# A trunk of two decoder layers on one core: the order of copies, low parts and differences in the last round of the down projection

## The chip, the cores and the metric

The kernel runs on one core of a Trainium2 chip. The core's engines work side by side, each through its own list of instructions in a fixed order: TensorE (PE in the profile) multiplies matrices, VectorE (DVE), ScalarE (ACT) and GpSimd (POOL) do elementwise work, and SyncE (SP) issues the transfers. An engine that waits at the head of its list holds up everything behind it. The metric is the time of one execution in device microseconds, as the median of several runs.

## The reference

The model has a Mamba-2 layer and a layer of stick-breaking attention. Each is followed by a gated feed-forward block (FFN). Only the end of that block, its down projection, is touched here. It takes 2816 features of about 1040 tokens to 1024 features, once in each layer.

```python
D_MODEL = 1024
SEQ = 1024
D_FF = 256 * ((8 * D_MODEL // 3 + 255) // 256)   # 2816

def _conv_ffn(u, w_up, conv_w, conv_b, w_down):
    h = _causal_dwconv(u @ w_up, conv_w, conv_b)
    g, val = jnp.split(h, 2, axis=-1)
    return (jax.nn.silu(g) * val) @ w_down

def reference(x, ...):
    ...
        h = h + _conv_ffn(_rmsnorm(h, ffn_norm[layer]), ffn_w_up[layer], ffn_conv_w[layer],
                          ffn_conv_b[layer], ffn_w_down[layer])
    return _rmsnorm(h, final_norm)[:, N_META:]
```

## The kernel before

**Three products for one.** Every operand in float32 is kept as a high part, which is a rounded copy made on ACT, and a low part, which is the operand less the high part. `mm3` (lines 194 to 200) multiplies high by high (L198), high by low (L199) and low by high (L200) into one bank of PSUM. The low part of a weight is made on POOL by `pieces` in four instructions of 256 columns (all on L99); the low part of the tokens' operand is made on DVE.

**The down projection.** The 22 blocks of 128 features are treated in two ways. Sixteen blocks go through a scheme that makes a two by two block product out of seven smaller ones, after sums and differences of the operands (products 1, 2, 7, 6, 5, 3, 4 in this order). There are two rounds, and a round has two sets (`Set`) of two feature blocks in each half. A product is multiplied for the first set and then for the second into the same banks, and after the second set DVE adds each bank to its running sum in `add` (L1383; in the first round ACT copies some of them). Layer 0 has 1040 tokens: a product there has eight tiles of 260 columns, which take all eight banks. Layer 1 has 1024 tokens (the meta tokens are gone): four tiles of 512 columns, so that two products fit in the banks. The other six blocks, the "plain rows" (`rows`), are multiplied in the usual way behind the last product: for the first quarter of the tokens (`j == 0`) all six rows go into the eight banks at once (`wide_first`), and then DVE adds them to the stream on L1467.

**The operands.** `operands(i)` makes what a product needs of one set. DVE forms a sum or difference of weights or of tokens (L1320, output `w` or `b`). ACT copies the weights' high part (`wh`, L1327) and the tokens' high part (`gh`, L1329). POOL makes `wl`; DVE makes `gl` (L1330). Product 4 has one difference, of tokens (b21 less b11). `make` calls this one set ahead of the multiplication in the program's text. The tiles `wh` and `wl` have three buffers each, so the last product's operands can be copied only when TensorE has left a product in front.

**The plain rows' operands.** `weights(b, hi, lo)` loads a row's weights into a `w32` tile (L1390), copies the high part on ACT (L1391), and makes the low part on POOL. Row 0 and row 1 take the buffers `fh` and `fl`, in which the second set's raw weights lie, row 2 an `x32` tile, row 3 two large tiles, and rows 4 and 5 `wh` and `wl`. `w32` has three buffers. Row 0 is called at product 3, the others at product 4. `tokens(0)` loads the six rows' tokens of the first half (L1401), copies their high part on ACT (L1402, output `g`), and makes the low part on DVE (L1403). `tokens(1)` does it for the second half behind the first quarter.

**The sums.** When all seven products are there, `sums` puts them together into the result in 28 additions on DVE (L1349), each asked for by `next(work)`: two behind each of the six plain rows of the first quarter, then one behind each of the eight feature tiles of the second and third quarters. In layer 0 POOL also scales and splits the first weights of the attention (`first_key`, `load_w`, lines 176 to 185) while this goes on.

**What sets the order.** Outside the attention a planner orders the instructions of each engine, and the queue of transfers too. It goes by the place of an instruction in the program's text and by times that it models, and it hands out a tile's buffers as they come free in these modelled times. `behind(a, b, reason)` ties `a` behind `b` in that order. A tie between instructions of one engine adds no wait of its own to the program; it fixes which comes first.

Of the kernel before, what the change touches and what calls it, by code (L numbers as in the profile page):

```python
# [13 lines left out]
P = 128  # L14
# [75 lines left out]
def pieces(eng, out, x, y, op):  # L90

    n = out.shape[1]
    size = 1
    for d in out.shape[2:]:
        size *= d
    step = max(1, PIECE // size)
    for a in range(0, n, step):
        c = slice(a, min(a + step, n))
        eng.tensor_tensor(out[:, c], x[:, c], y[:, c], op=op)  # L99


class Trunk:
# [1168 lines left out]
    def down(self, layer, gd, hd, pool, after, each=None):  # L1271
# [9 lines left out]
        half = lambda j: slice(S - S * j, 2 * S - S * j)  # L1281

        behind = self.behind
        lows = []

        def behind_low(ins, n):

            if len(lows) >= n:
                behind(ins, lows[-n], "behind the low part in front")
# [4 lines left out]
        class Set:  # L1294
# [16 lines left out]
            def operands(me, i):  # L1311

                b, w = me.b, me.w
                b11, b12, b21, b22 = b[0, 0], b[0, 1], b[1, 0], b[1, 1]
                a11, a12, a21, a22 = w[0, 0], w[0, 1], w[1, 0], w[1, 1]
                a = {7: (a21, a11, a21, SUB), 6: (a21, a22, a21, SUB), 5: (a11, a11, a21, ADD), 3: (a21, a12, a21, SUB)}.get(i)
                b = {7: (b12, b22, b12, SUB), 6: (b11, b11, b12, ADD), 5: (b12, b22, b11, SUB), 4: (b11, b21, b11, SUB)}.get(i)
                for x, n in ((a, 2), (b, 1)):
                    if x:
                        d = tt(*x[:3], op=x[3])  # L1320
# [6 lines left out]
                nc.scalar.activation(wh, y, AF.Copy)  # L1327
                pt(wl, y, wh.bitcast(F32), op=SUB)
                nc.scalar.activation(gh, x, AF.Copy)  # L1329
                lows.append(tt(gl, x, gh.bitcast(F32), op=SUB))  # L1330
                return gh, gl, wh, wl

# [44 lines left out]
        def add(i, f, t, ps, first):  # L1377
            s0, n = wide[t]
            x = acc[i, f][:, s0 : s0 + n]
            if first and i in (1, 5, 6, 7):  # L1380
                nc.scalar.activation(x, ps[:, :n], AF.Copy)
            else:
                self.last_add = tt(x, x, ps[:, :n], op=ADD)  # L1383

        rows = range(2 * NW, KF)
        ws, us = [], {}

        def weights(b, hi, lo):
            w32 = self.wp.tile([P, 1024], F32, tag="w32", name=self.nm("w32"))
            nc.sync.dma_start(w32, a["w_down"][layer, b])  # L1390
            nc.scalar.activation(hi, w32, AF.Copy)  # L1391
            pt(lo, w32, hi.bitcast(F32), op=SUB)
            ws.append((hi, lo))

        def tokens(x):

            us[x] = []
            for b in rows:
                t = self.Q("g", F32R)
                hi, lo = t[:, :S], t[:, QW // 2 : QW // 2 + S]  # L1400
                nc.sync.dma_start(lo.bitcast(F32), gd[b, :, S * x : S * x + S])  # L1401
                nc.scalar.activation(hi, lo.bitcast(F32), AF.Copy)  # L1402
                low = tt(lo, lo.bitcast(F32), hi.bitcast(F32), op=SUB)  # L1403
# [18 lines left out]
        for m in range(0, len(plan), 2):  # L1422
            r, i, _ = plan[m]
            last = r + 1 == len(rounds)
            ps = {}
            if r == 0 and i == 2:
                for f in range(KD):
                    nc.sync.dma_start(h[f][:, : 2 * S] if f < 4 else h[f][:, half(0)], hd[f] if f < 4 else hd[f, :, half(0)])
            if last and i == 4:
                h22 = [self.Q("h22") for _ in range(2)]  # L1430
                h22 = [h22[f // 2][:, f % 2 * S : f % 2 * S + S] for f in range(4)]
                for f in range(4):
                    nc.sync.dma_start(h22[f], hd[4 + f, :, half(1)])
            for x in range(2):
                make(m + x + 1)
                if last and i == 3 and x:
                    weights(rows[0], *own())
                if last and i == 4 and not x:
                    tokens(0)
                    weights(rows[1], *own())  # L1440
                    weights(rows[2], *(pool.tile([P, QW], F32R, tag="x32", name=self.nm(z))[:, :D] for z in ("wh", "wl")))
                    weights(rows[3], *(self.Q(z, F32R)[:, :D] for z in ("wh", "wl")))
                    for b in rows[4:]:
                        weights(b, *common())
                for n, (t, f) in enumerate((t, f) for t in range(len(wide)) for f in range(4)):
                    if x == 0:
                        ps[t, f] = kinds[(m // 2 * 4 * len(wide) + n) % 8]("acc")
                    part(ps[t, f], made[m + x], f, t, x == 0)
                    if x == 1:
                        add(i, f, t, ps.pop((t, f)), r == 0)  # L1450
                del made[m + x]
        banks = cycle((self.mm, self.mm, self.ex, self.lg, self.lg))
        res, work = None, sums()
        for j in range(4):
            out = h if j > 1 else h[:4] + h22
            wide_first = [bank("acc") for bank in kinds] if j == 0 else []
            for i, (hi, lo) in enumerate(us[0] if j == 0 else ()):
                for f, ps in enumerate(wide_first):
                    wh, wl = (w[:, f * P : f * P + P] for w in ws[i])
                    self.mm3(ps[:, :FN], wh, wl, hi[:, :FN], lo[:, :FN], i == 0, i == len(ws) - 1)  # L1460
                ahead = token_lows[min(i + 2, len(ws) - 1)]
                for _ in range(2):
                    next(work, None)
                ahead = None
            for f in range(KD):
                if j == 0:
                    self.last_add = tt(out[f][:, :FN], out[f][:, :FN], wide_first[f][:, :FN], op=ADD)  # L1467
# [467 lines left out]
```

## Time and profile before

| what | before |
|---|---|
| median of 3 runs | 2886.41 us (2883.43 to 2888.3) |
| the profiled execution's own time | 2883.7 us |
| its span, first to last instruction | 2882.0 us |
| PE busy | 2828.9 us, 98% of the span |
| DVE busy | 2093.5 us, 73% |
| ACT, POOL busy | 1629.0 us, 57%; 1622.6 us, 56% |
| mean granted TensorE clock | 0.997 |

The profile was taken in one execution of its own. Rows of the timeline give the start from the beginning of the span in us, the duration in us, the engine, the line of the program, the operation, the output and inputs by their names with shapes, and the count where like neighbours are merged; in square brackets stands how long the engine was idle ahead of the row, and what ended that. TensorE's matmuls overlap in the record: one of 260 columns is shown with 0.28 us, but the next starts 0.12 us after it, so the time of a stretch is read from starts. A few per cent of the matmul records can be missing.

### The profile page before, as it was taken

What the parts mean: (1) busy time and instruction counts of PE and PEld (TensorE: products, weight loads), DVE (VectorE), ACT (ScalarE), POOL (GpSimd) and SP (SyncE); (2) the same over time, 40 slices, a digit from 0 to 9 for tenths busy, and PEclk for the clock granted to TensorE, in tenths of its full rate; (3) what the DMA queues carried; (4) which work ended last, traced back from release to release, by engine and by line L of the source; (5) the groups of instructions that cost most, each with busy time, mean ns of one, the idle gap of its engine ahead of it and who ended that gap; (6) DMA issues with size and microseconds to landing.
All of it is one profiled execution on the core that took longest, in us unless ns stands there. A gap on an engine that the chain in (4) does not pass through costs nothing. (4 is left out here: it accounts for less than half of the span.)

```text
span 2882.0 us, 58690 instructions
## 1 busy us (share of the span) xinstructions
PE 2828.9 (98%) x21859; PEld 2712.8 (94%) x21859; DVE 2093.5 (73%) x4068; ACT 1629.0 (57%) x3393; POOL 1622.6 (56%) x2440
## 2 busy tenths in 40 slices
PE   8999999999999999999999999999999999999998
PEld 7989999999999999999999999999798999999888
DVE  5676666668596767676886888888759676667776
ACT  5555454543265655555335888887736555565433
POOL 2366455643529888868843222222363888886872
PEclk9999999999999999999999999999999999999999
DMA  4233334333412222244132222221332222225331
GB/s 118 85 112 99 112 87 134 104 131 104 131 55 97 76 80 80 78 169 156 53 121 72 65 62 69 62 59 53 135 117 76 80 82 81 75 81 183 110 103 67
DMA packets 135674, 274.51 MB, mean 95 GB/s; under 512 B 15859, under 2 KB 68220, under 8 KB 135388
## 3 DMA queue, kind: packets, MB, share of 16 engines
q1 hardware_dynamic: 129764, 259.60, 28.7%
q0 software_dynamic: 2048, 6.49, 0.6%
q10 hardware_dynamic: 3576, 4.67, 0.5%
q8 instruction: 172, 2.82, 0.4%
q14 instruction: 114, 0.93, 0.1%
HBM read 204.63 MB, written 51.16 MB: 89 GB/s over the span
## 5 line engine op out<-in xcount | busy, mean ns | idle before, releaser
L99 POOL TENSOR_TENSOR wl<-w,wh 128x256 fp32r<-128x256 f32 x768 | 685.0, 922 | 366.5 <-ACT wh L185 268.0
L198 PE MATMUL pj<-uh,wh 128*128 128x348 f32 (+2 forms) x1536 | 501.2, 327 | 4.0 <-DVE qs L1573 1.9
L199 PE MATMUL pj<-ul,wh 128*128 128x348 f32 (+2 forms) x1536 | 495.1, 322 | 0.2 <-DVE ul L309 0.2
L200 PE MATMUL pj<-uh,wl 128*128 128x348 f32 (+2 forms) x1536 | 491.8, 320 | 0.0
L198 PE MATMUL p<-bh,fh 128*128 128x262 f32 (+1 forms) x1408 | 401.1, 285 | 5.7 <-DVE p L1222 5.5
L200 PE MATMUL p<-bh,fl 128*128 128x262 f32 (+1 forms) x1408 | 400.9, 285 | 1.0 <-POOL fl L99 1.0
L199 PE MATMUL p<-bl,fh 128*128 128x262 f32 (+1 forms) x1408 | 398.4, 283 | 0.1
L99 POOL TENSOR_TENSOR fl<-x,fh 128x256 fp32r<-128x256 f32 x352 | 264.9, 784 | 189.6 <-ACT fh L1159 163.6
L199 PE MATMUL p<-bl,wh 128*128 128x262 f32 (+1 forms) x1040 | 295.5, 284 | 1.6 <-DVE bl L1083 1.6
L198 PEld LDWEIGHTS pj<-uh,wh 128*128 128x128 f32 x1536 | 288.8, 188 | 7.9 <-issue 2.0
L198 PE MATMUL p<-bh,wh 128*128 128x262 f32 (+1 forms) x1040 | 295.1, 284 | 0.4 <-ACT ft L1219 0.4
L200 PE MATMUL p<-bh,wl 128*128 128x262 f32 (+1 forms) x1040 | 294.4, 283 | 0.0
L199 PEld LDWEIGHTS pj<-ul,wh 128*128 128x128 f32 x1536 | 289.4, 188 | 1.8 <-DVE ul L309 0.7
L200 PEld LDWEIGHTS pj<-uh,wl 128*128 128x128 f32 x1536 | 288.9, 188 | 0.1
L328 DVE SCALAR_TENSOR_TENSOR c<-p,params,c 128x260 f32<-128x260 f32 (+1 forms) x528 | 248.4, 480 | 54.5 <-ACT c L325 48.1
L198 PEld LDWEIGHTS p<-bh,fh 128*128 128x128 f32 x1408 | 268.0, 190 | 6.6 <-DVE p L1222 5.9
L199 PEld LDWEIGHTS p<-bl,fh 128*128 128x128 f32 x1408 | 268.3, 191 | 0.5 <-DVE bl L1083 0.4
L200 PEld LDWEIGHTS p<-bh,fl 128*128 128x128 f32 x1408 | 267.1, 190 | 1.6 <-POOL fl L99 1.3
L1219 ACT ACTIVATE ft<-p 128x262 f32<-128x262 f32 (+1 forms) x352 | 133.2, 382 | 178.4 <-DVE p L1222 110.2
L200 PE MATMUL acc<-gh,wl 128*128 128x260 f32 (+1 forms) x672 | 214.5, 321 | 3.0 <-POOL wl L99 2.9
L199 PE MATMUL acc<-gl,wh 128*128 128x260 f32 (+1 forms) x672 | 214.8, 321 | 0.0
L198 PE MATMUL acc<-gh,wh 128*128 128x260 f32 (+1 forms) x672 | 211.5, 321 | 3.1 <-DVE h L1383 3.0
(344 smaller groups left out, 7915.1 us busy)
## 6 DMA issues: line engine op xcount, KB each, us to landing
w<-in_w_up SPq DMA_DIRECT2D x88, 512.0 KB
w<-in_w_down SPq DMA_DIRECT2D x44, 512.0 KB
w<-in_w_in SPq DMA_DIRECT2D x40, 512.0 KB
E<-ea_d SPq DMA_DIRECT2D x32, 464.0 KB
D<-acs_d SPq DMA_DIRECT2D x32, 420.5 KB
g<-c SPq DMA_DIRECT2D x88, 130.0 KB
g<-c SPq DMA_DIRECT2D x88, 128.0 KB
b<-g SPq DMA_DIRECT2D x16, 520.0 KB
```

What stands on the lines that cost most here:

```text
L99: eng.tensor_tensor(out[:, c], x[:, c], y[:, c], op=op)
L198: self.behind(mm(out, wh, uh, start=first, stop=False, skip_group_check=joins), tie, "behind the sums of squares")
L199: mm(out, wh, ul, start=False, stop=False, skip_group_check=joins)
L200: self.last_mm = mm(out, wl, uh, start=False, stop=last, skip_group_check=joins)
L328: ins = nc.vector.scalar_tensor_tensor(out, ps[:, o + i : o + i + n], wcol(i), out, op0=ALU.mult, op1=ALU.add)
L1219: nc.scalar.activation(s[:, :N], ps[:, :N], AF.Copy)
```

## The change

In the last round of both layers' down projection:

- `pieces` returns its instructions, and `add` keeps the last round's sums of each product in `adds`.
- The difference of tokens for product 4 is tied behind sums of product 5 on DVE: for the first set behind the sum a quarter of the way through the product's sums (the 2nd of 8 in layer 0, the 1st of 4 in layer 1), for the second set behind the one at three quarters (the 6th of 8, the 3rd of 4).
- Row 0 of the plain rows is only loaded at product 3 (`fetch`); its copy and low part stand in the text at product 4, behind `tokens(0)`, with the other rows'.
- All six rows' copies are tied in a chain on ACT behind the last product's last `wh`, and their low parts in a chain on POOL behind the last product's last `wl`.
- The copies in `tokens(0)` are tied behind the last product's last `gh` on ACT. Its low parts are tied behind sums of product 3 on DVE: in layer 0 behind the 2nd, 4th, 6th, and the last three behind the 8th; in layer 1 behind the 1st, 2nd, 3rd, and the others behind the 4th.
- Behind the sixth plain row no sums are asked for. The two that stood there are asked for in the second quarter, at feature tiles 3 and 7.

Nothing of the computation changes; the number of instructions is the same.

```diff
 def pieces(eng, out, x, y, op):
...
+    done = []
     for a in range(0, n, step):
         c = slice(a, min(a + step, n))
-        eng.tensor_tensor(out[:, c], x[:, c], y[:, c], op=op)
+        done.append(eng.tensor_tensor(out[:, c], x[:, c], y[:, c], op=op))
+    return done
...
-        lows = []
+        lows, adds, copied, split = [], {}, [], []
...
                         behind_low(d, n)
+                        if x is b and i == 4 and 5 in adds:
+                            behind(d, adds[5][(me.k % 4 + 1) * len(adds[5]) // 4 - 1], "behind the sums of the product in front")
...
-                nc.scalar.activation(wh, y, AF.Copy)
-                pt(wl, y, wh.bitcast(F32), op=SUB)
-                nc.scalar.activation(gh, x, AF.Copy)
+                copied[:] = [nc.scalar.activation(wh, y, AF.Copy)]
+                split[:] = pt(wl, y, wh.bitcast(F32), op=SUB)[-1:]
+                self.last_copy = nc.scalar.activation(gh, x, AF.Copy)
...
                 self.last_add = tt(x, x, ps[:, :n], op=ADD)
+                if not first:
+                    adds.setdefault(i, []).append(self.last_add)
...
-        def weights(b, hi, lo):
+        def fetch(b):
             w32 = self.wp.tile([P, 1024], F32, tag="w32", name=self.nm("w32"))
             nc.sync.dma_start(w32, a["w_down"][layer, b])
-            nc.scalar.activation(hi, w32, AF.Copy)
-            pt(lo, w32, hi.bitcast(F32), op=SUB)
+            return w32
+
+        def weights(w32, hi, lo):
+            high = nc.scalar.activation(hi, w32, AF.Copy)
+            behind(high, copied[-1], "behind the copies in front")
+            low = pt(lo, w32, hi.bitcast(F32), op=SUB)
+            behind(low[0], split[-1], "behind the low parts in front")
+            copied.append(high)
+            split.append(low[-1])
             ws.append((hi, lo))
...
-                nc.scalar.activation(hi, lo.bitcast(F32), AF.Copy)
+                high = nc.scalar.activation(hi, lo.bitcast(F32), AF.Copy)
                 low = tt(lo, lo.bitcast(F32), hi.bitcast(F32), op=SUB)
                 token_lows.append(low)
                 if x:
                     behind(low, self.last_add, "behind the first tile")
+                else:
+                    n = len(adds[3])
+                    behind(high, self.last_copy, "behind the products' copies")
+                    behind(low, adds[3][min((len(us[x]) + 1) * n // 4, n) - 1], "behind the products' sums")
...
                 if last and i == 3 and x:
-                    weights(rows[0], *own())
+                    row0 = fetch(rows[0]), *own()
                 if last and i == 4 and not x:
                     tokens(0)
-                    weights(rows[1], *own())
...
+                    weights(*row0)
+                    weights(fetch(rows[1]), *own())
...
-                for _ in range(2):
+                for _ in range(2 if i + 1 < len(ws) else 0):
                     next(work, None)
...
-                if j:
+                for _ in range(2 if j == 1 and f % 4 == 3 else 1 if j else 0):
                     next(work, None)
```

More of the change, by code (lines that the diff above doesn't have):

```diff
@@ L1436, in down @@
                 if last and i == 3 and x:
-                    weights(rows[0], *own())
+                    row0 = fetch(rows[0]), *own()
                 if last and i == 4 and not x:
                     tokens(0)
-                    weights(rows[1], *own())
-                    weights(rows[2], *(pool.tile([P, QW], F32R, tag="x32", name=self.nm(z))[:, :D] for z in ("wh", "wl")))
-                    weights(rows[3], *(self.Q(z, F32R)[:, :D] for z in ("wh", "wl")))
+                    weights(*row0)
+                    weights(fetch(rows[1]), *own())
+                    weights(fetch(rows[2]), *(pool.tile([P, QW], F32R, tag="x32", name=self.nm(z))[:, :D] for z in ("wh", "wl")))
+                    weights(fetch(rows[3]), *(self.Q(z, F32R)[:, :D] for z in ("wh", "wl")))
                     for b in rows[4:]:
-                        weights(b, *common())
+                        weights(fetch(b), *common())
                 for n, (t, f) in enumerate((t, f) for t in range(len(wide)) for f in range(4)):
```

## The prediction

> **What bounds the kernel now.** I read the page first, then who kept TensorE waiting in the last round of each layer's down projection, then the timelines of the four engines there.
>
> ```profile
> span 2882.0 us, 58690 instructions
> PE 2828.9 (98%) x21859; PEld 2712.8 (94%) x21859; DVE 2093.5 (73%) x4068; ACT 1629.0 (57%) x3393; POOL 1622.6 (56%) x2440
> ```
>
> TensorE is busy for 98% of the span. The change adds or removes no matmul, so all it can give is time in which TensorE waits or runs slowly at the places it touches. Those are two: 1425 to 1480 us (layer 0) and 2760 to 2815 us (layer 1). TensorE's waits there, first layer 0 (two rows), then layer 1:
>
> ```profile
> PE acc L198 <- DVE h L1383: 3.0, 4, 1.1
> PE acc L198 <- DVE h L1467: 1.2, 1, 1.2
> ...
> PE acc L200 <- POOL wl L99: 2.9, 3, 1.3
> ```
>
> The waits come to 7.1 us, but a wait costs more than its idle time, since the pipeline refills behind it. The full loss follows from starts in TensorE's timeline. Products 3 and 4 run from the first row of each pair to the second, in the order: layer 0 first round, layer 0 last round, layer 1 first round, layer 1 last round.
>
> ```profile
> 1348.46 0.28 PE L198 MATMUL acc<-gh,wh 128*128 128x260 f32 x1
> 1371.44 0.28 PE L198 MATMUL acc<-gh,wh 128*128 128x260 f32 x1
> ...
> 1429.08 0.28 PE L198 MATMUL acc<-gh,wh 128*128 128x260 f32 x1
> 1456.57 0.28 PE L198 MATMUL acc<-g,fh 128*128 128x260 f32 x1
> ...
> 2689.24 0.39 PE L198 MATMUL acc<-gh,wh 128*128 128x512 f32 x1
> 2711.61 0.39 PE L198 MATMUL acc<-gh,wh 128*128 128x512 f32 x1
> ...
> 2767.36 0.39 PE L198 MATMUL acc<-gh,wh 128*128 128x512 f32 x1
> 2794.88 0.28 PE L198 MATMUL acc<-g,fh 128*128 128x256 f32 x1
> ```
>
> The same matmuls take 22.98 us in layer 0's first round and 27.49 in its last: 4.51 lost. In layer 1 it is 22.37 and 27.52: 5.15 lost. These two numbers are what the ties can win; one product for one set is 22.98 / 4 = 5.74 us (layer 0) or 22.37 / 4 = 5.59 (layer 1).
>
> **Part 1, layer 0, DVE (ties of the differences and of the tokens' low parts).** TensorE's waits, then DVE's rows around them:
>
> ```profile
> 1431.38 0.39 PE L198 MATMUL acc<-gh,wh 128*128 128x260 f32 x1 [1.05 <-DVE h L1383]
> 1443.59 0.36 PE L198 MATMUL acc<-gh,wh 128*128 128x260 f32 x1 [1.10 <-DVE h L1383]
> ```
>
> ```profile
> 1426.78 0.41 DVE L1383 TENSOR_TENSOR h<-h,acc 128x260 f32<-128x260 f32 x1
> ...
> 1429.22 1.77 DVE L1320 TENSOR_TENSOR b<-b,b 128x1040 f32<-128x1040 f32 x1
> 1430.91 1.75 DVE L1383 TENSOR_TENSOR h<-h,acc 128x260 f32<-128x260 f32 x5
> 1432.59 1.49 DVE L1330 TENSOR_TENSOR gl<-b,gh 128x1040 fp32r<-128x1040 f32 x1
> ...
> 1438.93 4.18 DVE L1403 TENSOR_TENSOR g<-g 128x520 fp32r<-128x520 f32 x4 [4.17 <-ACT g L1402]
> 1443.03 1.42 DVE L1383 TENSOR_TENSOR h<-h,acc 128x260 f32<-128x260 f32 x4
> 1446.25 0.79 DVE L1403 TENSOR_TENSOR g<-g 128x520 fp32r<-128x520 f32 x1 [1.80 <-ACT g L1402]
> ```
>
> At 1431.38 product 3 needs the second bank of product 5, but DVE was making product 4's difference (1429.22) ahead of that sum. At 1443.59 product 4 needs a bank of product 3: DVE stood idle for 4.17 us for a copy of the tokens and then made four low parts, with product 3's sums queued behind them. The other two waits are of this kind, behind the fifth and sixth low parts. All eight banks are in use, so a sum has about one product, 5.1 us, from the end of its tile until its bank is needed.
>
> With the ties the 2nd sum of product 5 stands ahead of the first difference, and the 6th ahead of the second. A difference is 1.77 us, `gl` behind it 1.49, so a sum is late by some 3 us at most, less than 5.1. The tokens' low parts then come in one or two between product 3's sums (4.18 us for four, beside POOL), the last three behind its 8th. What is late next is the low parts themselves: the last one at about 1445 in place of 1448, while the plain rows start at 1452. That is covered. I take the whole 4.51 us. Bounds: 1.0 us may stay if a token's transfer lands late and holds a sum (the row of the chain of waits below has 3.71 us for it; the transfers stand in SP's queue, where row 2's load, waiting for product 4's first `wl`, may now stand in front of them); nothing beyond 4.51 can be won.
>
> ```profile
> 1441.84 3.71 DMA g<-g
> ```
>
> **Part 2, layer 1, ACT and POOL (chains of copies and low parts).** TensorE, then ACT, then POOL:
>
> ```profile
> 2769.40 0.50 PE L200 MATMUL acc<-gh,wl 128*128 128x512 f32 x1 [0.73 <-POOL wl L99]
> 2780.95 0.50 PE L200 MATMUL acc<-gh,wl 128*128 128x512 f32 x1 [0.87 <-POOL wl L99]
> 2783.24 0.50 PE L200 MATMUL acc<-gh,wl 128*128 128x512 f32 x1 [1.32 <-POOL wl L99]
> ```
>
> ```profile
> 2761.22 1.05 ACT L1327 ACTIVATE wh<-w 128x1024 fp32r<-128x1024 f32 x1
> ...
> 2773.88 1.06 ACT L1391 ACTIVATE fh<-w 128x1024 fp32r<-128x1024 f32 x1 [3.97 <-POOL wl L99]
> 2775.33 1.06 ACT L1391 ACTIVATE wh<-w 128x1024 fp32r<-128x1024 f32 x1 [0.39 <-DMA w<-in_w_down]
> 2776.30 1.04 ACT L1327 ACTIVATE wh<-w 128x1024 fp32r<-128x1024 f32 x1
> ```
>
> ```profile
> 2760.45 4.81 POOL L99 TENSOR_TENSOR fl<-w,fh 128x256 fp32r<-128x256 f32 x4 [1.17 <-ACT fh L1391]
> 2765.23 8.62 POOL L99 TENSOR_TENSOR wl<-w,wh 128x256 fp32r<-128x256 f32 x8
> 2776.47 11.13 POOL L99 TENSOR_TENSOR wl<-w,wh 128x256 fp32r<-128x256 f32 x12 [2.63 <-ACT wh L1391]
> ```
>
> Row 0's low part (2760.45, 4.81 us) stands ahead of product 3's `wl`, and TensorE waits 0.73 for it. Then ACT stands idle for 3.97 us at row 1's copy, copies rows 1 and 2, and only at 2776.30 product 4's `wh`. POOL's twelve pieces from 2776.47 begin with row 2's four; product 4's follow, and TensorE waits 0.87 and 1.32.
>
> Without row 0, product 3's `wl` can start when its `wh` is there, at 2762.3, three us earlier. Product 4's `wh` can be copied when ACT is free at about 2769.9, 6.4 us earlier, its `wl` is then done by 2776.7 at the latest, and TensorE wants it at 2778.5. The waits go, and the slow stretch behind them too:
>
> ```profile
> 2783.78:2787.19 3.41, 3.41 (x9) 2.65 (x8) 2.14 (x4) 2.21 (x3) 3.41 (x5) 0.50 0.53 196
> ```
>
> This is the row of that stretch: its granted clock is 0.50, so 3.41 us of it did 1.7 us of work. The 5.15 us are 2.92 of waits, 1.7 of half clock and 0.5 of refilling. I take all 5.15; bounds 5.15 and, if the clock falls for a reason of its own, 3.45. The Trainium skill, "TensorE: Matmul & The Clock Gate", Part 1, says that the clock falls after an idle window of about 3.4 us; the waits here were 0.87 and 1.32 us, so by that rule they did not cause the fall, it would stay, and the sum would be 1.7 us smaller. I go by the row, which begins right behind these waits.
>
> What is late next: all six rows' low parts now follow the last product's. It can be copied when TensorE has left product 3's first set (about 2773), so its `wl` is done by about 2780. A row's four pieces take 2.8 us alone, 4.8 beside DVE. Rows reach TensorE from 2789.7, one each 2.8 us. The loads chain too: rows 3, 4 and 5 take the `w32` buffers of rows 0, 1 and 2. A load takes 5.25 us at worst:
>
> ```profile
> 2770.07 5.25 DMA w<-in_w_down
> ```
>
> Row 2's low part is done by about 2790, row 5 lands at 2795, its copy and low part end by 2800, and TensorE needs it at 2803.7: cost nothing, with 3.7 us of cover. In layer 0 the same count gives about 1458 against 1466.4.
>
> **Part 3, layer 0, the first quarter of the plain rows.** DVE, then POOL:
>
> ```profile
> 1457.11 12.09 DVE L1349 TENSOR_TENSOR p<-p 128x520 f32<-128x520 f32 x3
> ...
> 1474.62 2.75 DVE L1467 TENSOR_TENSOR h<-h,acc 128x260 f32<-128x260 f32 x8
> ```
>
> ```profile
> 1460.02 4.61 POOL L99 TENSOR_TENSOR w<-w,params 128x256 f32<-128x256 f32 x8
> 1464.60 2.82 POOL L99 TENSOR_TENSOR wl<-w,wh 128x256 fp32r<-128x256 f32 x4
> ```
>
> Twelve of the 28 sums stand between 1457.11 and 1474.62. Three take 12.09 us, the other nine 5.4, so 0.61 each, and the first took 12.09 - 1.22 = 10.87. It ended 0.56 us after POOL's unbroken run did (1464.60 + 2.82 = 1467.42). The other eleven stood between it and the first addition of L1467, and TensorE waited 1.2 us for that (the second row of waits; 1.4 with the refill). In layer 1, at the same place and with POOL running, it did not happen:
>
> ```profile
> 2795.68 3.25 DVE L1349 TENSOR_TENSOR p<-p 128x512 f32<-128x512 f32 x3
> ```
>
> The change takes two sums (1.2 us) from in front of L1467, but TensorE gets there 4.5 us earlier, at 1469.2 (1475.1 less 1.4 less 4.5). If the first sum is let through, ten sums of about 1.2 are done by 1465: the wait goes, -1.4. If it is held again, POOL's end counts. Its work is the same and starts earlier, but waits for loads; I estimate 1466. Ten sums then end at 1472.0, TensorE waits about 3.2: +1.8 net. With POOL no earlier than now it is 4.7 of wait, +3.3, and perhaps 1.7 for a half clock: +5.0. One of the two meetings in the trace was held, so I take the middle of -1.4 and 1.8, +0.2. The Trainium skill, "SBUF — State Buffer", section "Who interferes with whom", says a DVE instruction with two SBUF inputs is blocked by a GpSimd instruction that reads SBUF for the whole of that instruction. By this a sum would wait for one POOL piece, some 0.7 us, and the term would be -1.4; the 10.87 us, over some fifteen pieces, says otherwise.
>
> The sums put off to tiles 3 and 7 of the second quarter are 2 x 0.61 us on DVE there, beside 2 us of TensorE for each tile: nothing.
>
> **Sum.** -4.5 - 5.15 + 0.2 = -9.5 us. The profiled execution took 2883.7 us (span 2882.0), 2.7 below the median of 2886.4. I carry the difference over to the median: 2886.4 - 9.5 = 2877 us (-0.33%).
>
> **Rivals.**
> A. *The rows' low parts become the wait.* All 24 pieces stand behind the last product. If DVE runs beside POOL all the time at 1.19 us a piece, they take 28.6 us: from about 1439 to 1467.6 against 1466.4, from 2777 to 2805.6 against 2803.7. That is 1.2 and 1.9 of wait, up to 1.7 of half clock for each: 6.5 us lost of the 9.5, 2883.4 us. For it: the 11.13 us of twelve pieces in layer 1. Against: the last rows' pieces run at 0.70 apart (2.82 for four).
> B. *Slower: DVE is held on a token's low part.* As in part 3, but at the first one tied between product 3's sums of layer 0 (about 1437), with product 3's other sums queued behind. POOL's run is unbroken from the last product's `wl` until it waits for row 5's load, about 1457: 20 us. The banks give 5 of these, so TensorE waits 15, and 1.7 for the clock: -9.5 + 16.7 = +7.2, 2893.6. From a hold of about 13 us it is slower than before. For it: the 10.87 us. Against: the four low parts at 1438.93 took turns with POOL (4.18 for four).
> C. *The ties change nothing that counts.* The planner goes by modelled times; if it puts something else in front (a row's load on SP, a copy on ACT), the waits move but stay: 2886.4. Against it: ties fix exactly the orders that the rows above show.
>
> **How the numbers follow.** Forecast 0.60, A 0.20, B 0.12, C 0.08. Within 0.2% (5.8 us, about what a measurement here can tell from no change) lie A and C, with a little of B: same 0.28; slower 0.12. The range: the lowest is 4.5 + 5.15 + 1.4 = 11.1 off, 2875.3, less 3 for the spread of runs, 2872. Upward it takes in A and C with 2 us of spread, 2888.5; B lies outside. The forecast's own range is 2872 to 2881.
>
> **What would show it.** Right: products 3 and 4 of the last round take about 23.0 and 22.4 us; no stretch at clock 0.50 near 2784; on ACT no row's copy (L1391) ahead of the last L1327; on DVE sums of product 3 between the tokens' low parts. Part 3 is told by the first L1349 of layer 0 and the wait at L1467. Wrong: a wait on `fl` or `wl` behind the last product (A), a row of L1330 or L1403 of many us (B), or waits of the same length elsewhere (C).

## The result, and the profile after

The changed kernel takes 2874.49 us in the median of 7 runs (2873.28 to 2878.03), the kernel before, beside it, 2882.89 (2881.04 to 2888.3): 8.4 us less, a ratio of 0.9967 with a 95% interval of 0.9956 to 0.9977. A later comparison gave 2874.20 against 2881.06, ratio 0.9982 (0.9973 to 0.9992). The ratios here and below are those on record, which are not quotients of the medians.

The first lines of the changed kernel's page (its ten more entries lie outside the engines' counted work):

```profile
span 2874.9 us, 58700 instructions
## 1 busy us (share of the span) xinstructions
PE 2827.0 (98%) x21859; PEld 2713.8 (94%) x21859; DVE 2095.8 (73%) x4068; ACT 1629.9 (57%) x3393; POOL 1623.1 (56%) x2440
```

Line numbers have moved: `mm3` is now L200 to L202, the products' weight copy L1331, a row's copy L1400, the tokens' copy and low part L1415 and L1416, the products' sums L1387, the 28 sums L1353. Each run below has its own line numbers. From TensorE's timeline, the start of product 3 in the last round and the first matmul of the plain rows, layer 0 and then layer 1:

```profile
1429.00 0.28 PE L200 MATMUL acc<-gh,wh 128*128 128x260 f32 x1
1452.08 0.29 PE L200 MATMUL acc<-g,fh 128*128 128x260 f32 x1
...
2765.72 0.39 PE L200 MATMUL acc<-gh,wh 128*128 128x512 f32 x1
2788.08 0.28 PE L200 MATMUL acc<-g,fh 128*128 128x256 f32 x1
```

The two products take 23.08 us (27.49 before) and 22.36 (27.52). TensorE waits for nothing in either stretch, nor behind the first quarter of the plain rows. ACT in layer 0, before and then after:

```profile
1435.41 1.06 ACT L1391 ACTIVATE fh<-w 128x1024 fp32r<-128x1024 f32 x1 [3.25 <-POOL wl L99]
1436.38 1.05 ACT L1327 ACTIVATE wh<-w 128x1024 fp32r<-128x1024 f32 x1
1437.33 1.04 ACT L1391 ACTIVATE wh<-w 128x1024 fp32r<-128x1024 f32 x1
1438.27 2.21 ACT L1402 ACTIVATE g<-g 128x520 fp32r<-128x520 f32 x4
```

```profile
1429.12 1.06 ACT L1331 ACTIVATE wh<-w 128x1024 fp32r<-128x1024 f32 x1 [1.40 <-PE acc L201]
1430.84 1.07 ACT L1333 ACTIVATE gh<-b 128x1040 fp32r<-128x1040 f32 x1 [0.65 <-DVE b L1322]
1432.43 1.28 ACT L1415 ACTIVATE g<-g 128x520 fp32r<-128x520 f32 x2 [0.52 <-DMA g<-g]
1434.89 1.06 ACT L1331 ACTIVATE wh<-w 128x1024 fp32r<-128x1024 f32 x1 [1.17 <-PE acc L201]
1435.86 1.99 ACT L1400 ACTIVATE fh<-w 128x1024 fp32r<-128x1024 f32 x2
```

Before, ACT stood 3.25 us at row 1's copy, whose buffer POOL was still reading, with product 4's weights and all tokens behind it. After, the products' copies and the tokens' go first, and the tokens start 5.8 us earlier. Not all of that is ACT's: in the changed kernel the tokens' copy waits for its own load (`DMA g<-g`), which comes earlier too (`e8` below). DVE then, after: the tokens' low parts between product 3's sums, and later the first of the 28 sums:

```profile
1436.75 1.27 DVE L1416 TENSOR_TENSOR g<-g 128x520 fp32r<-128x520 f32 x1
1437.95 0.75 DVE L1387 TENSOR_TENSOR h<-h,acc 128x260 f32<-128x260 f32 x2
...
1452.63 1.87 DVE L1353 TENSOR_TENSOR p<-p 128x520 f32<-128x520 f32 x2
```

The hold of 10.87 us is not there: two sums take 1.87 us. POOL, after:

```profile
1447.16 14.87 POOL L100 TENSOR_TENSOR wl<-w,wh 128x256 fp32r<-128x256 f32 x16
1461.99 5.54 POOL L100 TENSOR_TENSOR w<-w,params 128x256 f32<-128x256 f32 x8
1467.48 2.83 POOL L100 TENSOR_TENSOR wl<-w,wh 128x256 fp32r<-128x256 f32 x4
```

The rows' last low part ends at 1462.0, some 4 us before TensorE wants it, and POOL goes on to 1470.3, not to 1466 as estimated.

The stretches gained 4.41 + 5.16 us and the first quarter about 1.4, 11 in all, but the spans of the two profiled executions differ by 7.1. Starts of the same matmuls in both profiles tell where the rest is: 0.9 more is gained where the attention begins (`e4` below); lost are some 1.2 us in the rest of the attention, 3.0 from 2211 to 2271 us in layer 1's up projection and 0.9 in the rest of it. The up projection's instructions stand in the same order in both kernels. The changed kernel's profile has two waits there that the other lacks; the waits from 2180 to 2260 us:

```profile
PE p L200 <- ACT c L1212: 1.5, 1, 1.5
PE p L202 <- POOL fl L100: 1.0, 1, 1.0
PE p L200 <- ACT ft L1221: 0.8, 1, 0.8
```

Neither the first nor the third is in a second profile of the changed kernel (`r1` below), and each follows an addition on DVE that took far longer than its like, 4.44 us at 2220 and 5.16 at 2240 us, which that profile lacks too. I call this a hold, here and below any addition of over 3 us. The later one, then the end of the run of additions that POOL made meanwhile, and POOL's next instruction:

```profile
2239.97 5.16 DVE L1224 TENSOR_TENSOR ft<-ft,ft 128x258 f32<-128x258 f32 x1
```

```profile
2243.38 1.47 POOL L100 TENSOR_TENSOR x<-x,w 128x256 f32<-128x256 f32 x2
2248.74 0.74 POOL L100 TENSOR_TENSOR fl<-x,fh 128x256 fp32r<-128x256 f32 x1 [3.89 <-ACT fh L1161]
```

The addition ends at 2245.13, 0.28 us after POOL's run (2243.38 + 1.47). It looks like the long sum of the kernel before, which also ended shortly after POOL's run, in another place.

### The profile page after: what moved, and what is told of

Same layout as the page of the kernel before. It is cut to its first block, busy times and chain, and to the rows that moved or that the text cites. A ratio compares the mean times of both kernels' runs of the same rounds, so it can differ in the third digit from the quotient of the medians.

```text
span 2874.9 us, 58700 instructions
## 1 busy us (share of the span) xinstructions
PE 2827.0 (98%) x21859; PEld 2713.8 (94%) x21859; DVE 2095.8 (73%) x4068; ACT 1629.9 (57%) x3393; POOL 1623.1 (56%) x2440
## 4 chain that ended last, share of the span: by engine, by line
PE 89%; DVE 5%; ACT 2%; POOL 2%; issue 1%; DMA 1%; DVEq 0%; SPq 0%; ACTq 0%; POOLq 0%
PE p L200 9%; PE p L202 9%; PE p L201 9%; PE acc L200 8%; PE acc L201 8%; PE acc L202 8%; PE pj L200 8%; PE pj L201 8%; PE pj L202 8%; PE po L1681 3%; PE lg L1640 2%; PE wT L1667 2%; PE y L799 1%; PE S L788 1%; PE y L801 1%
## 5 line engine op out<-in xcount | busy, mean ns | idle before, releaser
L200 PE MATMUL pj<-uh,wh 128*128 128x348 f32 (+2 forms) x1536 | 501.1, 327 | 3.1 <-DVE xbc L330 1.4
L202 PE MATMUL pj<-uh,wl 128*128 128x348 f32 (+2 forms) x1536 | 492.1, 321 | 0.0
L200 PE MATMUL p<-bh,fh 128*128 128x262 f32 (+1 forms) x1408 | 400.9, 285 | 7.2 <-DVE p L1224 5.5
L202 PE MATMUL p<-bh,fl 128*128 128x262 f32 (+1 forms) x1408 | 400.8, 285 | 1.0 <-POOL fl L100 1.0
L200 PE MATMUL p<-bh,wh 128*128 128x262 f32 (+1 forms) x1040 | 295.7, 284 | 1.2 <-ACT ft L1221 1.2
L200 PEld LDWEIGHTS pj<-uh,wh 128*128 128x128 f32 x1536 | 288.8, 188 | 6.5 <-ACT xbc L327 1.7
L202 PE MATMUL p<-bh,wl 128*128 128x262 f32 (+1 forms) x1040 | 294.1, 283 | 0.0
L202 PEld LDWEIGHTS pj<-uh,wl 128*128 128x128 f32 x1536 | 288.9, 188 | 0.1
L200 PEld LDWEIGHTS p<-bh,fh 128*128 128x128 f32 x1408 | 267.8, 190 | 8.3 <-DVE p L1224 5.9
L202 PEld LDWEIGHTS p<-bh,fl 128*128 128x128 f32 x1408 | 266.6, 189 | 1.7 <-POOL fl L100 1.3
L202 PE MATMUL acc<-gh,wl 128*128 128x260 f32 (+1 forms) x672 | 213.3, 319 | 0.0
L200 PE MATMUL acc<-gh,wh 128*128 128x260 f32 (+1 forms) x672 | 210.8, 320 | 0.1
```

Of the source, the lines that this page charges most:

```text
L200: self.behind(mm(out, wh, uh, start=first, stop=False, skip_group_check=joins), tie, "behind the sums of squares")
L202: self.last_mm = mm(out, wl, uh, start=False, stop=last, skip_group_check=joins)
```

## The experiments

The measure is the time of products 3 and 4 of the last round in each layer, from starts in TensorE's timeline; the total time tells less, since its differences are near its spread. The stretch does not count a wait in front of its first matmul.

| run | layer 0, us | layer 1, us | median, us | ratio to the kernel before, 95% interval |
|---|---|---|---|---|
| before, profile | 27.49 | 27.52 | 2882.89 | |
| changed | 23.08 | 22.36 | 2874.49 | 0.9967 (0.9956 to 0.9977) |
| e3, rows as before | 28.76 | 23.70 | 2876.82 | 0.9979 (0.9970 to 0.9988) |
| e2, no token ties | 23.08 | 22.36 | 2878.68 | 0.9979 (0.9968 to 0.9990) |
| e1, no tie of differences | 23.11 | 22.25 | 2874.38 | 0.9963 (0.9951 to 0.9976) |
| e4, twelve sums | 23.09 | 22.27 | 2875.89 | 0.9970 (0.9958 to 0.9981) |
| e5, rows' part alone | 23.11 | 22.23 | 2874.86 | 0.9967 (0.9955 to 0.9980) |
| e7, chain of low parts alone | 26.78 | 22.23 | 2878.32 | 0.9980 (0.9971 to 0.9989) |
| e8, chain of copies alone | 23.12 | 22.24 | 2875.34 | 0.9972 (0.9960 to 0.9984) |
| v1, pauses everywhere | 23.09 | 22.36 | 2880.80 | 0.9986 (0.9977 to 0.9995) |
| before, again (r0) | 27.48 | 25.85 | 2881.19 (one run) | |
| changed, again (r1) | 23.08 | 22.36 | 2874.20 | 0.9982 (0.9973 to 0.9992) |
| v2, pauses in the up projection | 23.09 | 22.36 | 2874.20 | 0.9976 (0.9967 to 0.9985) |

**e3: the rows' part undone.**

```diff
-                    row0 = fetch(rows[0]), *own()
+                    weights(fetch(rows[0]), *own())
-                    weights(*row0)
-            behind(high, copied[-1], "behind the copies in front")
-            behind(low[0], split[-1], "behind the low parts in front")
```

> The changed kernel with the plain rows' copies and low parts as they were: row 0 again at product 3, no chains behind the last product. Measure: products 3 and 4 of the last round (the changed kernel has 23.08 us in layer 0 and 22.36 in layer 1, the kernel before 27.49 and 27.52). Theory: layer 1's loss was the rows' work in front of the products' low parts, and the half clock followed from it: layer 1 goes back to about 27.5 us, with waits on POOL's low part of 0.7, 0.9 and 1.3 us and a stretch at clock 0.50 behind them; layer 0 stays within 0.5 us of 23.1. Rival 1 (the clock falls for a reason of its own): the waits come back without the slow stretch, 25.8 us. Rival 2 (ties on DVE did it all): layer 1 stays at 22.4. Time: 5 us above the changed kernel, 2879.5; rival 1 2878, rival 2 2874.5.

Layer 1 took 23.70 us, 1.3 more than the changed kernel and not 5.1; layer 0, which should have stayed, took 28.76, longer than in the kernel before. TensorE's waits, layer 0 and layer 1, then ACT and DVE in layer 0:

```profile
1445.79 0.58 PE L200 MATMUL acc<-gh,wh 128*128 128x260 f32 x1 [2.53 <-DVE h L1387]
...
2782.60 0.50 PE L202 MATMUL acc<-gh,wl 128*128 128x512 f32 x1 [1.14 <-POOL wl L100]
```

```profile
1435.04 1.06 ACT L1400 ACTIVATE wh<-w 128x1024 fp32r<-128x1024 f32 x1 [5.47 <-DMA w<-in_w_down]
...
1437.90 1.06 ACT L1333 ACTIVATE gh<-b 128x1040 fp32r<-128x1040 f32 x1
...
1443.44 1.35 ACT L1413 ACTIVATE g<-g 128x520 fp32r<-128x520 f32 x2 [3.54 <-DMA g<-g]
```

```profile
1444.11 1.28 DVE L1414 TENSOR_TENSOR g<-g 128x520 fp32r<-128x520 f32 x1 [2.64 <-ACT g L1413]
```

ACT stands 5.47 us at a row's copy for its load, with product 4's `wh` and `gh` behind it. The tokens' copies come 11 us later than in the changed kernel, and ACT waits 3.54 us for their own loads, which are issued only at 1439.45, behind a row's load (in the changed kernel at 1429.19). The ties on DVE, all in place, keep the first sums in front, but DVE waits for the late copy, and TensorE 2.53 us for the next sum. So the rows' part holds up layer 0 too, through ACT and through the queue of transfers, and the ties on DVE don't mend it. The 28.76 us also hold 6.83 us at half clock (last section), worth 3.4; this execution took 2881.24 us, 4.4 above the run's median.

In layer 1 the other edits alone bring most of the gain: 23.70 us is 3.8 below the first profile of the kernel before and 2.15 below its second (`r0`). Which of them does it, no run tells.

**e2: the tokens' ties taken out.**

```diff
-                else:
-                    n = len(adds[3])
-                    behind(high, self.last_copy, "behind the products' copies")
-                    behind(low, adds[3][min((len(us[x]) + 1) * n // 4, n) - 1], "behind the products' sums")
```

> The changed kernel without the ties of the tokens' copies and low parts. Theory: DVE makes several tokens' low parts in front of product 3's sums again; layer 0's products 3 and 4 take 2.8 us more (25.9), with waits on those sums of 1.1, 0.7 and 0.2 us at product 4; layer 1 stays at 22.4, where a product has banks to spare. Rival: the rows' chain on ACT alone brings the tokens' copies early enough, so that nothing waits: 23.1 in layer 0. Time: 2.8 us above the changed kernel, 2877.3; rival 2874.5.

23.08 and 22.36 us: the rival was right, these ties win nothing here. The median was 4.2 us above the changed kernel's while both stretches were the same. The profiled execution lost its time elsewhere: behind a hold of 5.56 us at 878 us TensorE waits 3.9 us for ACT, and by the starts of the matmuls that place cost some 5 us. A second hold, of 6.15 us at 2791, brought no wait.

**e1: the tie of product 4's differences taken out.**

```diff
-                        if x is b and i == 4 and 5 in adds:
-                            behind(d, adds[5][(me.k % 4 + 1) * len(adds[5]) // 4 - 1], "behind the sums of the product in front")
```

> The changed kernel without the tie of product 4's differences behind product 5's sums. Theory: the second difference stands in front of five of product 5's sums again, TensorE waits about 1.0 us for a bank at product 3's first set; layer 0's products 3 and 4 take 1.4 to 1.7 us more (24.6 to 24.8); layer 1 stays at 22.4. Rival: with the rows' copies gone from ACT the first difference's operand is earlier and the sums come in time: 23.1. Time: 1.6 us above the changed kernel, 2876.1; rival 2874.5.

23.11 us, with one wait of 0.32 us at the first matmul of product 3. The tie is worth some 0.3 us where 1.4 to 1.7 were expected. Elsewhere it goes with a loss: the same 2900 matmuls of layer 1's up projection, from about 2280 us on, take 349.2 us or more in the seven profiles with this tie and 348.3 to 348.6 in the six without it. The instructions stand in the same order and no wait is listed; the cause stays open.

**e4: the two sums put back.**

```diff
-                for _ in range(2 if i + 1 < len(ws) else 0):
+                for _ in range(2):
-                for _ in range(2 if j == 1 and f % 4 == 3 else 1 if j else 0):
+                for _ in range(1 if j else 0):
```

> The changed kernel with two sums behind the sixth plain row again (twelve in the first quarter) and one for each tile of the second. Theory: the 10.87 us hold of a sum in the kernel before was a chance meeting of DVE and POOL, and only it made TensorE wait at L1467; twelve sums of 1.2 us beside POOL end at about 1466, before the first quarter does (1467): no wait of TensorE behind the first quarter, first quarter as long as in the changed kernel. Rival: the sixth row's two sums cost by themselves: a wait of about 1.2 us at the first matmul of the second quarter in layer 0. Time: 2874.5 against 2875.7.

No wait behind the first quarter: the theory held. But the two sums do count later. Where layer 0's attention begins, TensorE waits for `qs` on DVE, first in the changed kernel, then in this one:

```profile
PE pj L200 <- DVE qs L1591: 0.9, 1, 0.9
...
PE pj L200 <- DVE qs L1591: 1.7, 1, 1.7
```

All seven profiles with the sums moved have 0.8 or 0.9 us there, all six without have 1.7. So moving them wins 0.8 us in a place that neither the prediction nor the measure above looks at.

These four point to the rows' part as the one that counts for the two products, with the reserve made for layer 1. Three kernels built on that part test it.

**e5: the rows' part alone** (the edits of e1, e2 and e4 together).

> The kernel before with the plain rows' part of the change alone: row 0's copy and low part behind the others' place in the text, the chain of copies on ACT, the chain of low parts on POOL. No tie of tokens' copies and low parts, none of product 4's differences, twelve sums in the first quarter. New theory after the first four runs: this part is the whole change. Products 3 and 4 of the last round take 23.1 to 23.5 us in layer 0 and 22.4 in layer 1, and the time is the changed kernel's, 2874.5 within 2. Rival (the ties on DVE are needed, one stands in for the other): layer 0 takes over 24.5 us, with a wait of 1 us or more on a sum of product 5 or 3.

23.11 and 22.23 us, 2874.86 us in the median: in the two products everything that the change gives, but for 0.3 us in front of product 3. DVE in layer 0:

```profile
1433.32 3.23 DVE L1414 TENSOR_TENSOR g<-g 128x520 fp32r<-128x520 f32 x4 [0.69 <-ACT g L1413]
1436.47 1.17 DVE L1385 TENSOR_TENSOR h<-h,acc 128x260 f32<-128x260 f32 x3
```

Four low parts stand in front of product 3's sums, as in the kernel before. There they began at 1438.93, here at 1433.32, and they are done before the sums' banks are wanted. The order on DVE was nearly harmless; its input was late.

**e7: the chain of low parts without the chain of copies** (e5 less one line).

```diff
-            behind(high, copied[-1], "behind the copies in front")
```

> As the one with the rows' part alone, but without the chain of copies on ACT: only the low parts are tied, on POOL. Theory: ACT's list is what was wrong. A row's copy that waits for its buffer or its load stands in front of product 4's weight copy and of the tokens' copies; a tie on POOL can't mend that, and may make it worse. Products 3 and 4 take 25 us or more in layer 0 and 23.5 or more in layer 1, and the time is 2877 or more. Rival (POOL's order was what counted): 23.1 and 22.4, 2874.5.

Layer 0 as expected, 26.78 us; layer 1 not: 22.23, no wait. The two longest of four waits in layer 0, and ACT there:

```profile
1432.08 0.39 PE L200 MATMUL acc<-gh,wh 128*128 128x260 f32 x1 [1.43 <-DVE h L1385]
1443.77 0.36 PE L200 MATMUL acc<-gh,wh 128*128 128x260 f32 x1 [0.60 <-DVE h L1385]
```

```profile
1435.40 1.06 ACT L1398 ACTIVATE fh<-w 128x1024 fp32r<-128x1024 f32 x1 [2.54 <-POOL wl L100]
1436.37 1.04 ACT L1329 ACTIVATE wh<-w 128x1024 fp32r<-128x1024 f32 x1
1438.60 2.02 ACT L1412 ACTIVATE g<-g 128x520 fp32r<-128x520 f32 x3 [1.19 <-DMA g<-g]
```

In layer 0 a row's copy is back in front of product 4's, and the tokens are as late as before; the last 1.19 us of that ACT waits for their loads. In layer 1 the kernel before had POOL's order wrong too (row 2's low part ahead of product 4's), and there the tie on POOL is enough. Row 0's new place in the text stands here as well and does nothing on ACT by itself: its copy starts at 1421.49 and 2760.22 us, as early as in the kernel before (1420.79 and 2759.31). The tie on POOL does not move a whole low part, though: only the first of the four pieces is tied, and POOL ran row 0's other three at 2761.36, long before the first at 2783.68.

**e8: the chain of copies without the chain of low parts** (e5 less the other line).

```diff
-            behind(low[0], split[-1], "behind the low parts in front")
```

> As the one with the rows' part alone, but without the chain of low parts on POOL: only the copies are tied, on ACT. Theory: a low part can't come before its copy, so POOL's order follows from ACT's, and the chain of low parts adds nothing: 23.1 to 23.5 us in layer 0, 22.4 in layer 1, 2874.5. Rival (POOL takes a row's low part in front of the last product's wl): a wait on POOL of 0.5 us or more at product 4's second set, 23 or more in layer 1.

23.12 and 22.24 us, 2875.34 us: of the ties, the chain of copies alone (with row 0's place in the text) does it all for the two products, in both layers.

It does not act on ACT alone, since the planner orders the queue of transfers too. The issues of the tokens' first four loads in layer 0 (`SPq` marks SyncE's issues), in the kernel before and in this one:

```profile
1431.61 0.33 SPq L1390 DMA_DIRECT2D w<-in_w_down  x1
1432.03 2.40 SPq L1401 DMA_DIRECT2D g<-g  x4
...
1429.05 3.41 SPq L1411 DMA_DIRECT2D g<-g  x4
```

Before, a row's load stands in front of the tokens' loads; with the chain they come first, 3 us earlier, and ACT's first copy of the tokens starts when its load has landed (1433.10, 5.2 us earlier). What ACT's order is worth and what the queue's, no run separates.

**The kernel before again**, to see what in its first profile was chance.

> The kernel before once more, for a second profile. Theory: its waits in the last round are the order's and come again (layer 0's products 3 and 4 in 27.5 us, layer 1's in 27.5 or, if the two waits of product 4 fall otherwise into the clock's count, 25.8); the hold of 10.87 us on the first sum is chance, so the first quarter of layer 0's plain rows has no wait behind it this time, and there is a hold of 4 to 6 us in the up projection, as in seven of the eight profiles of kernels with the change or parts of it. Rival: the hold belongs to the order of the kernel before, and stands at the first sum again.

The waits came again to within 0.1 us. In layer 1:

```profile
2768.54 0.50 PE L200 MATMUL acc<-gh,wl 128*128 128x512 f32 x1 [0.74 <-POOL wl L99]
2779.99 0.50 PE L200 MATMUL acc<-gh,wl 128*128 128x512 f32 x1 [0.79 <-POOL wl L99]
2782.27 0.50 PE L200 MATMUL acc<-gh,wl 128*128 128x512 f32 x1 [1.32 <-POOL wl L99]
```

But the granted clock stayed at 1.00 behind them (the row of that stretch), and the two products took 25.85 us instead of 27.52:

```profile
2783.00:2787.00 4.00, 4.00 (x19) 3.22 (x18) 3.28 (x5) 2.82 (x4) 3.92 (x5) 1.00 0.43 147
```

The traces show why the same waits can end in two ways. In each of the thirteen profiles every stretch at half clock between the program's start and its end lasts 3.41 or 6.83 us, and they begin whole multiples of 3.41 us apart: the clock changes on a grid of steps. Where the waits fall on the grid differs. The step ahead of the fall in the first profile, then the two steps in this one (length, then TensorE's busy time):

```profile
2780.37:2783.78 3.41, 1.50 (x5) 0.97 (x6) 2.82 (x3) 0.01 (x1) 3.41 (x4) 1.00 0.81 267
...
2777.50:2780.91 3.41, 2.62 (x11) 1.54 (x9) 3.41 (x4) 1.92 (x3) 3.41 (x4) 1.00 0.17 55
2780.91:2784.32 3.41, 2.09 (x10) 1.70 (x10) 1.92 (x3) 1.20 (x3) 3.41 (x6) 1.00 0.77 270
```

In the first profile nearly all of both waits lies in one step, 1.91 us idle, and the next step is slow. Here the boundary at 2780.91 parts them, 0.79 and 1.32 us idle, and no slow step follows.

On DVE the first sums took their usual time, TensorE did not wait behind the first quarter, and a hold stood in the up projection of layer 0 instead:

```profile
896.43 4.65 DVE L1222 TENSOR_TENSOR ft<-ft,ft 128x262 f32<-128x262 f32 x1
...
1457.59 3.04 DVE L1349 TENSOR_TENSOR p<-p 128x520 f32<-128x520 f32 x3
```

So two of the things that the first profile showed, the half clock of layer 1 (1.7 us) and the wait at L1467 (1.4 us), belong to that execution and not to the kernel.

**Pauses against the holds.** v1 gives POOL a pause inside each low part, sum or difference:

```diff
+        gap = self.cp.tile([P, 4], F32, tag="gap", name="gap")
+        def pause(ins):
+            rest = nc.gpsimd.memset(gap, 0.0)
+            self.behind(rest, ins, "behind the piece in front")
+            return rest
...
+        if rest is not None:
+            tie(ins, rest)
+        rest = pause(ins) if len(done) % 2 else None
```

> The changed kernel with a pause in POOL's runs: behind the first and third of the four pieces of every low part (and every second of eight) POOL sets 4 columns of a tile of its own to zero, about 0.1 us without reading anything. Theory: when DVE's instruction with two operands in SBUF meets POOL's next piece within a few hundredths of a us, DVE is held until POOL's unbroken run ends (10.87, 4.4, 5.2, 5.6, 5.8, 6.2 us in the six profiles so far); with pauses no hold is over 2.5 us, the waits of 1 to 1.5 us that they cause in the up projection go, and the time falls by 1 to 3 us, to 2872 to 2873.5. Rival (the hold doesn't end at a pause, or the pauses cost POOL more than they give): holds of over 2.5 us stay, and the time is the changed kernel's or up to 5 us more.

No DVE instruction of that profile took over 2.5 us: no hold. (The close starts that the theory names do not show: at the sixteen holds of the other profiles the nearest start of a POOL addition is 0.01 to 0.29 us away.) But the time rose to 2880.8 us. The planner made another order of the up projection's start, and its waits from 2180 to 2260 us now have

```profile
PE p L219 <- POOL gap L131: 1.9, 1, 1.9
PE p L217 <- ACT fh L1178: 1.2, 1, 1.2
```

with a stretch of 6.83 us at half clock that begins behind the second, at 2202 us. v2 keeps one pause in each group of pieces, in the up projection alone and from its third block on, so that the other engines' orders stay (TensorE's, ACT's and DVE's are the changed kernel's); the changed kernel ran beside it.

```diff
-        tt = lambda out, x, y, op: pieces(nc.gpsimd, out, x, y, op)
+        tt = lambda out, x, y, op: pieces(nc.gpsimd, out, x, y, op, b > 1)
...
+        rest = pause(ins) if pauses and len(done) == 2 else None
```

> The changed kernel with one pause of about 0.1 us (POOL sets 4 columns to zero) in the middle of the four pieces of each low part, sum and difference of the up projection's weights, from its third block on. The order of the other engines is unchanged. Theory: the earlier pauses lost because they changed the order and stood in front of pieces that TensorE waited for; these don't, and no hold in the up projection from the third block on is longer than 3.5 us. Each hold there cost TensorE 1 to 1.6 us, so the time is 1 to 2.5 us below the changed kernel beside it. Rival: the added instructions cost POOL as much as the holds cost, no difference.

> The changed kernel once more, on the same chip as the one with pauses in the up projection. Products 3 and 4 in 23.1 and 22.4 us again; the holds on DVE in the up projection stand at other or fewer places than in its first profile (2219 and 2240 us). Time 2874.5, within 2.

No hold in v2's profile, one of 4.64 us (at 897 us) in the changed kernel's, and 2874.20 us for both: no difference, as the rival said. Its reason, that the pauses cost what the holds cost, is not shown. By the starts of the matmuls the hold at 897 us costs 0.6 us, which the median can't tell, and no version here beats the changed kernel clearly.

## Why the prediction was right, and which of its steps were not

The forecast was 9.5 us less; 8.4 were measured, and 6.9 in the later comparison.

*Part 1, layer 0, 4.51 us by the ties on DVE.* The size was right (4.41), the cause was not. The step that failed is "DVE was making product 4's difference ahead of that sum", and likewise four low parts ahead of product 3's sums: I took what stood directly in front of the late sum for its cause. The same low parts in the same place do no harm in e5, where they start 5.6 us earlier. What counts is what stood in front of that input: the row's copy on ACT that waited for a buffer, with the products' and tokens' copies behind it, and the row's load in the queue of transfers, with the tokens' loads behind it. That the size came out right is luck: another edit than the one credited mends this. Part 2 describes this for layer 1; in layer 0's own rows DVE's idle 4.17 us ended by a copy of the tokens said it too, and I did not follow that copy back. e8 shows that the chain of copies (with row 0's place) is enough, e2 that the tokens' ties add nothing beside it, e1 that the tie of the differences adds 0.3 us.

*Part 2, layer 1, 5.15 us.* The forecast of the first profile's loss was right to 0.01 us, and the waits were named rightly: rows' work in front of the products'. Two points were not. The 1.7 us of half clock are not in each execution (25.85 us in the second profile of the kernel before), since they hang on where the waits fall on the clock's steps; without them the term is 3.5 us. And I gave ACT and POOL an equal part: in layer 1 either chain is enough alone (e7, e8), and the other edits without the rows' part already bring most of it (e3); in layer 0 only the chain of copies is enough.

*Part 3, the first quarter, +0.2 us.* The held sum was rightly read as a meeting of DVE with POOL's run, but not as a thing that moves between executions of one kernel. Among the other profiles it stood at layer 0's first sum only in e3, with 3.17 us, and at layer 1's only in e2, with 6.15. Without a hold the term is about nil. Had the sum been held, the wait would by the prediction's own count have been longer than the upper bound's 4.7 us, which has POOL end at 1467.4; it ended at 1470.3.

*The sum.* Without what the first profile had by chance it is 4.4 + 3.5 = 7.9 us, which two profiles show directly (27.48 and 25.85 against 23.08 and 22.36), between the two measured differences. The forecast was too high by what one execution had by chance. It also left out the 0.8 us won at the attention (e4) and the 0.6 to 0.9 lost in layer 1's up projection with the tie of the differences (e1); that these nearly cancel is luck.

*The rivals.* A did not come: no wait for a row's low part, the last of layer 0's done 4 us ahead. B did not come: no low part of a token was held in the thirteen profiles, though e3 shows how much DVE's ties can cost when their input is late. C is refuted by the stretches.

## What to carry to other kernels

Follow a late instruction back through every engine before naming its cause: the instruction directly in front of it may only have been pushed there by a wait two engines away. Work that is needed later belongs behind work that is needed now on the engine that executes in order and first has to wait for a buffer or a load; here, with row 0's place in the text, one chain of ties on ACT did for the two products what five edits did together. A tie in a planned order can move other engines' lists and the queue of transfers as well, so look at them all before the gain is put down to one. Before a term of a sum rests on a single event, such as a slow stretch or one long instruction, see whether a second profile has it.

## What the runs showed of the hardware that was not expected

A DVE addition with both operands in SBUF that meets POOL's run of back-to-back additions can be held over many of POOL's instructions: 10.87, 5.16, 4.65 us and others, in all profiles but the two with pauses. Of the sixteen holds (additions of over 3 us) fourteen ended 0.28 to 0.56 us after POOL's run. They come back at few places: five at about 896 us and six at about 2240, in the two up projections. In most other meetings the two took turns at 1.2 us each. The Trainium skill, "SBUF — State Buffer", section "SBUF: two separate sides", has the loser blocked for the whole instruction of the winner; these runs show it blocked for some fifteen. With pauses of POOL of 0.1 us that read nothing, no hold showed in v1 and v2.

TensorE's clock fell to half behind waits of 0.87 and 1.32 us that lay almost whole in one step of 3.41 us, and stayed up behind 0.79 and 1.32 us that lay in two (r0). It fell behind a single wait of 1.25 us in v1, and in a wait of 2.53 us (e3), of which 1.78 lay in the step ahead of the fall; it did not behind waits of 1.43 (e7) and 1.14 us (e3), nor behind the first of two steps that share a wait of 3.7 us in r1, with 1.78 us idle. So the idle time of the step alone does not settle it. The row of the slow stretch in e3:

```profile
1445.03:1451.86 6.83, 6.08 (x28) 6.08 (x29) 6.83 (x12) 4.43 (x6) 6.75 (x7) 0.50 0.51 185
```

The Trainium skill, "TensorE: Matmul & The Clock Gate", Part 1, names an idle window of about 3.4 us; in these runs steps that were idle for a part were enough, though not always.
